# A hybrid encoder block on one core: half of the first feed-forward product by seven block products instead of eight

## The chip, the core and the metric

The kernel runs on one core of one Trainium2 chip. A core has TensorE (PE, matrix products into PSUM), VectorE (DVE), ScalarE (ACT), GpSimd (POOL) and SyncE (SP), each with a queue of instructions that it works through in order, and 16 DMA engines. The metric is the device time in microseconds, as the median of several runs.

## What is computed

One layer on x of 256 rows by 2048 columns, float32: a normalisation, two mixing branches (retention and latent attention) with gates, an output product, and then the feed-forward part that this case is about:

```python
z = _rmsnorm(h, norm_mlp_g[l]) @ w_up[l]          # 256 x 2048 by 2048 x 8192
h = h + jnp.square(jax.nn.relu(z)) @ w_down[l]    # 256 x 8192 by 8192 x 2048
...
return _rmsnorm(h, norm_f_g)
```

## The kernel before

**How a product is made.** TensorE multiplies float32 numbers in a form (`float32r`) that keeps fewer bits, so each operand is split: `hi` is the value cast to that form by ACT, `lo` is the rest, value minus hi, subtracted by DVE. A product is then three: hi by hi, hi by lo, lo by hi. `split` (L214 on) and `weights` (L145 to L153) do this; `weights` first loads a block of 128 x 1024 weights (512 KB) into a `raw` tile with a DMA in SP's queue, casts it on ACT (L151) and subtracts on DVE (L152). The pool `wp` has 5 raw, 4 hi and 4 lo tiles. Every weight is used once, so these steps accompany the whole kernel.

**The first feed-forward product** (w_up, L785 to L800) takes its input transposed and split: `hT`, 16 blocks of 128 rows, each with hi and lo for the 256 rows of x side by side. It is made in 64 units of 128 output columns. A unit (`t_unit`) keeps a block of weights stationary: `t_pass1` (L159) multiplies w-hi by hi and lo of hT together, 512 columns in one matmul, 16 of them; `t_pass2` (L163) multiplies w-lo by hi, 256 columns, 16 of them. The two halves of the 512-column result are added by `joined` (ACT copy L206, DVE add L207), and one DVE operation (L800) makes max(z, 0) times z and stores it in `hid`. All of hid stays in SBUF, in four tiles of 16 KB per partition, three of them from the pool `act` of six such tiles. The first two units are begun in halves, because the last quarter of hT is transposed (`mlp_turn`, tile `ht`, L764) while they run.

**The second product** (w_down, `down`, L814 to L816) is the other way round: blocks of hid (split into `dh` and `dl`) are stationary, and 512 columns of w_down move, three matmuls for each of eight PSUM banks (`pd`, tile dn), over 64 blocks. Its last two blocks are kept back and done bank by bank, while the finishing normalisation starts. `hn`, the residual, stays in SBUF from the output product (w_out, tile wo, L199 to L202) to the end.

**What sets the order.** The program is written as straight code; a scheduler then orders the instructions of each engine by a simulated timeline and gives tiles their buffers as they come free. Waits between engines are semaphores. PSUM has eight banks of 512 columns, four in the pool `mm` and four in `at`.

Of the kernel before, what the change touches and what calls it, by code (L numbers as in the profile page):

```python
# [27 lines left out]
CHUNK = 64  # L28
DFF = 8192
FT = DFF // P  # L30
EPS = 1e-6
QK_SCALE = float(192.0 ** -0.5)
LOWEST = -3.4e38
# [55 lines left out]
def block_kernel(ctx: ExitStack, tc: tile.TileContext, A):  # L89
    nc = tc.nc  # L90
    V, SC, G, PE = nc.vector, nc.scalar, nc.gpsimd, nc.tensor
# [3 lines left out]
    cp = ctx.enter_context(tc.tile_pool(name="cp", bufs=1))  # L95
# [4 lines left out]
    def big(name, dt=F32, shape=(P, KT, S)):  # L100
        return act.tile(list(shape), dt, tag="act16", name=name)
# [31 lines left out]
    def mmps(name):  # L133
        return pmm.tile([P, 512], F32, tag="mm", name=name)
# [4 lines left out]
    uid = [0]  # L139
# [56 lines left out]
    def n_tile(out, w, x, t, k0, nk, start, stop):  # L196
# [4 lines left out]
        for k in range(nk):  # L201
            PE.matmul(out, x.hi(k0 + k, ts), w[1][:, k], start=False, stop=stop and k == nk - 1)  # L202

    def join(out, ps):
        t = sm.tile([P, S], F32, tag="join", bufs=2, name="join")
        SC.copy(t, ps[:, S:])  # L206
        V.tensor_tensor(out=out, in0=ps[:, :S], in1=t, op=ALU.add)  # L207
# [22 lines left out]
    warm = cp.tile([P, 1], F32, name="warm")  # L230
    SC.activation(warm, halfpi, AF.Copy)

    cold = cp.tile([P, 512], BF16, name="cold")
# [5 lines left out]
    rctx = ExitStack()  # L239
    rope_pool = rctx.enter_context(tc.tile_pool(name="rope", bufs=2))  # L240
    ictx = ExitStack()
    ip = ictx.enter_context(tc.tile_pool(name="ip", bufs=1))

# [8 lines left out]
    x = Pair("x")  # L252
# [12 lines left out]
    for k0, k1 in zip(LEAD_CHUNKS, LEAD_CHUNKS[1:]):  # L265
        n = k1 - k0
        hs = slice(k0 % HK, k0 % HK + n)
        if k0 % HK == 0:
            wt = [[wtile(kind, [P, HK, P]) for kind in ("hi", "lo")] for j in range(3)]
        t, o = lead_at(k0)  # L270
# [12 lines left out]
        for ps, (hi, lo) in zip(firsts, wt):  # L283
            w = hi[:, hs], lo[:, hs]
# [31 lines left out]
    ident = con[:, C_ID : C_ID + P]  # L316
# [33 lines left out]
    rxb = cp.tile([P, S], F32, name="rxb")  # L350
    V.tensor_copy(rxb, pb[:, :S])

    tabs = []
# [1 line left out]
    def table(j):  # L355
        ang, kk = angs[j]
        sgn = vec[:, V_INV + 2 + j : V_INV + 3 + j]
        own = ip if j == 0 else cp
        cos = own.tile([P, S], F32, name=f"cos{j}")
        sin = own.tile([P, S], F32, name=f"sin{j}")  # L360
# [157 lines left out]

    with ExitStack() as mctx:
        cc = big("cc", F32R, shape=(P, 2 * LT, 2, S))  # L520
        kpe = cp.tile([P, S], F32, name="kpe")
        lp = ExitStack()
        lpool = lp.enter_context(tc.tile_pool(name="lp", bufs=1))

# [232 lines left out]
    def mlp_turn(c):  # L757
        for jj in range(2):
            pT = atps(f"ht{c}{jj}")
            for j in range(2):  # L760
                kt = 4 * c + 2 * jj + j
                for t in range(2):
                    o = j * S + t * P
                    PE.transpose(pT[:, o : o + P], hn[:, t, kt * P : (kt + 1) * P], ident)  # L764
                g = vec[:, V_MLP + kt : V_MLP + kt + 1]
                split(hT.hi(kt), hT.lo(kt), pT[:, j * S : (j + 1) * S], scale=g)
    hp = ctx.enter_context(tc.tile_pool(name="hp", bufs=1))
    ssh = cp.tile([P, 2, 4], F32, name="ssh")
# [13 lines left out]
    V.tensor_scalar(rh2, rh2, 1.0 / D, EPS, op0=ALU.mult, op1=ALU.add)  # L782
    V.reciprocal(rh2, rh2)

    up = [mmps(f"z{i}") for i in range(2)]  # L785
    for i in range(2):
        t_half(up[i], A["w_up"][i], hT, 0)
        if i == 0:
            mlp_turn(3)
    hid = [big(f"hid{i}") for i in range(3)]  # L790
    hid.append(hp.tile([P, KT, S], F32, name="hid3"))
# [11 lines left out]
    ssf = cp.tile([P, 2, 68], F32, name="ssf")  # L803
    rf = cp.tile([P, 2], F32, name="rf")
    LAST = 2

    def down(i, t, c, w, hs):
        (hi, lo), (dh, dl) = w, hs
        ts = slice(t * P, (t + 1) * P)
        ws = slice(c % 2 * 512, c % 2 * 512 + 512)  # L810
        out = pd[t][c]
        end = i == FT - 1
        mm = tc.keep_in_program_order if i >= FT - LAST else (lambda ins: ins)
        mm(PE.matmul(out, dh[:, ts], hi[:, ws], start=i == 0, stop=False))  # L814
        mm(PE.matmul(out, dh[:, ts], lo[:, ws], start=False, stop=False))  # L815
        mm(PE.matmul(out, dl[:, ts], hi[:, ws], start=False, stop=end))  # L816

    tail = []
    for i in range(FT):
        dh = hp.tile([P, S], F32R, tag="dh", bufs=3, name=f"dh{i}")  # L820
        dl = hp.tile([P, S], F32R, tag="dl", bufs=3, name=f"dl{i}")
        split(dh, dl, hid[i // KT][:, i % KT])
        ws = []
        for half in range(2):
            w = weights(A["w_down"][i][:, half * 1024 : (half + 1) * 1024], [P, 1024])
            ws.append(w)
            if i < FT - LAST:
                for t in range(2):
                    for c in (2 * half, 2 * half + 1):
                        down(i, t, c, w, (dh, dl))  # L830
        if i >= FT - LAST:
            tail.append((i, ws, (dh, dl)))
# [7 lines left out]
    def finish(t, c, lo, hi, n):  # L840
        h = hn[:, t, c * 512 + lo : c * 512 + hi]
        ps = pd[t][c][:, lo:hi]
        V.scalar_tensor_tensor(h, in0=ps, scalar=rh2[:, t : t + 1], in1=h, op0=ALU.mult, op1=ALU.add)
        junk = hp.tile([P, 512], F32, tag="junk", bufs=2, name=f"junk{t}{n}")
# [32 lines left out]
def _t_units(w):  # L877
    k, n = w.shape
    return np.ascontiguousarray(w.reshape(k // P, P, n // P, P).transpose(2, 1, 0, 3))


def _n_units(w):
    k, n = w.shape
    u = w.reshape(k // 512, 4, P, n // 512, 512).transpose(3, 0, 2, 1, 4)
    return np.ascontiguousarray(u.reshape(-1, P, 4, 512))


def _cols(v):
# [57 lines left out]
```

## Time and profile before

| | us |
|---|---|
| median of three runs | 1631.58 (1631.27 to 1631.89) |
| the profiled execution | 1632.22 |
| its span, first to last instruction | 1630.4 |
| w_up in it, first z matmul to first dn matmul | 915.5 to 1272.7 |
| w_down and the end | 1272.7 to 1630.4 |
| mean granted TensorE clock | 0.998 of full |

The page of the profile gives busy times by engine, the chain of work that ended last, and groups of instructions by line, engine and tile. In a group's name `z<-hT,hi` means that tile z is written from hT and hi. A duration is that of one instruction; matmuls overlap, so their pace is read from the distance of their starts in the timeline.

### The profile page before, as it was taken

What the parts mean: (1) busy time and instruction counts of PE and PEld (TensorE: products, weight loads), DVE (VectorE), ACT (ScalarE), POOL (GpSimd) and SP (SyncE); (2) the same over time, 40 slices, a digit from 0 to 9 for tenths busy, and PEclk for the clock granted to TensorE, in tenths of its full rate; (3) what the DMA queues carried; (4) which work ended last, traced back from release to release, by engine and by line L of the source; (5) the groups of instructions that cost most, each with busy time, mean ns of one, the idle gap of its engine ahead of it and who ended that gap; (6) DMA issues with size and microseconds to landing.
All of it is one profiled execution on the core that took longest, in us unless ns stands there. A gap on an engine that the chain in (4) does not pass through costs nothing.

```text
span 1630.4 us, 23041 instructions
## 1 busy us (share of the span) xinstructions
PE 1614.9 (99%) x8782; PEld 1398.8 (86%) x8782; DVE 996.2 (61%) x1491; ACT 809.7 (50%) x1249; POOL 49.5 (3%) x62
## 2 busy tenths in 40 slices
PE   8999999999999999999999999999999999999997
PEld 6888888888889889888888888888888888888886
DVE  7974588655556658666765555555555555555555
ACT  6544555544445556765545544444444444444444
POOL 7100000000000000000000000000000000000001
PEclk9999999999999999999999999999999999999999
DMA  8665544555556554325575555555555655555553
GB/s 306 200 233 193 187 156 166 169 192 186 190 170 203 190 191 146 125 94 176 186 246 187 174 193 188 192 189 186 191 192 184 223 194 192 193 193 195 192 194 112
DMA packets 84480, 304.46 MB, mean 187 GB/s; under 512 B 9360, under 2 KB 9488, under 8 KB 83600
## 3 DMA queue, kind: packets, MB, share of 16 engines
q1 hardware_dynamic: 84368, 302.98, 55.3%
q8 instruction: 69, 1.13, 0.3%
q14 instruction: 43, 0.35, 0.1%
HBM read 300.84 MB, written 2.10 MB: 186 GB/s over the span
## 4 chain that ended last, share of the span: by engine, by line
PE 97%; DVE 1%; issue 0%; DMA 0%; ACT 0%; POOL 0%; SPq 0%; DVEq 0%; POOLq 0%; ACTq 0%
PE z L159 14%; PE z L163 8%; PE dn L816 7%; PE dn L814 7%; PE dn L815 7%; PE rg L159 4%; PE yr L159 4%; PE gr L159 4%; PE gm L159 4%; PE mo L159 4%; PE qk L159 2%; PE gr L163 2%; PE yr L163 2%; PE gm L163 2%; PE rg L163 2%; PE mo L163 2%
## 5 line engine op out<-in xcount | busy, mean ns | idle before, releaser
L152 DVE TENSOR_TENSOR lo<-raw,hi 128x1024 fp32r<-128x1024 f32 (+2 forms) x562 | 666.0, 1204 | 521.6 <-ACT hi L151 248.3
L151 ACT CAST hi<-raw 128x1024 fp32r<-128x1024 f32 (+2 forms) x562 | 580.8, 1035 | 536.9 <-PE z L159 135.2
L159 PE MATMUL z<-hT,hi 128*128 128x512 f32 x1024 | 245.5, 391 | 0.0
L159 PEld LDWEIGHTS z<-hT,hi 128*128 128x128 f32 x1024 | 188.0, 188 | 36.1
L815 PE MATMUL dn<-lo,dh 128*128 128x512 f32 x512 | 199.2, 389 | 0.0
L816 PE MATMUL dn<-hi,dl 128*128 128x512 f32 x512 | 199.2, 389 | 0.0
L814 PE MATMUL dn<-hi,dh 128*128 128x512 f32 x512 | 198.9, 389 | 0.0
L163 PEld LDWEIGHTS z<-hT,lo 128*128 128x128 f32 x1024 | 131.6, 191 | 5.1
L163 PE MATMUL z<-hT,lo 128*128 128x256 f32 x1024 | 133.1, 283 | 0.0
L815 PEld LDWEIGHTS dn<-lo,dh 128*128 128x128 f32 x512 | 96.1, 188 | 20.1
L816 PEld LDWEIGHTS dn<-hi,dl 128*128 128x128 f32 x512 | 96.1, 188 | 19.9
L814 PEld LDWEIGHTS dn<-hi,dh 128*128 128x128 f32 x512 | 96.1, 188 | 19.8
L216 ACT CAST dh<-hid 128x256 fp32r<-128x256 f32 x64 | 26.0, 407 | 89.3 <-PE dn L815 89.3
L159 PE MATMUL mo<-my,hi 128*128 128x512 f32 x256 | 65.5, 396 | 0.4 <-DVE val L207 0.4
L159 PE MATMUL rg<-x,hi 128*128 128x512 f32 x256 | 64.0, 395 | 0.0
L159 PE MATMUL yr<-ry,hi 128*128 128x512 f32 x256 | 61.4, 391 | 0.0
L159 PE MATMUL gr<-x,hi 128*128 128x512 f32 x256 | 61.3, 391 | 0.0
L159 PE MATMUL gm<-x,hi 128*128 128x512 f32 x256 | 61.1, 391 | 0.0
L159 PEld LDWEIGHTS gm<-x,hi 128*128 128x128 f32 x256 | 47.0, 188 | 9.1
L159 PEld LDWEIGHTS gr<-x,hi 128*128 128x128 f32 x256 | 47.0, 188 | 9.0
L159 PEld LDWEIGHTS yr<-ry,hi 128*128 128x128 f32 x256 | 46.9, 188 | 9.0
L159 PEld LDWEIGHTS rg<-x,hi 128*128 128x128 f32 x256 | 46.2, 188 | 8.6
(271 smaller groups left out, 2239.1 us busy)
## 6 DMA issues: line engine op xcount, KB each, us to landing
raw<-w_up SPq DMA_DIRECT2D x128, 512.0 KB, 4.2
raw<-w_down SPq DMA_DIRECT2D x128, 512.0 KB, 4.3
raw<-w_rv SPq DMA_DIRECT2D x32, 512.0 KB, 4.5
raw<-w_rg SPq DMA_DIRECT2D x32, 512.0 KB, 4.5
raw<-w_gret SPq DMA_DIRECT2D x32, 512.0 KB, 4.3
raw<-w_ret_o SPq DMA_DIRECT2D x32, 512.0 KB, 4.6
raw<-w_gmla SPq DMA_DIRECT2D x32, 512.0 KB, 4.4
raw<-w_out SPq DMA_DIRECT2D x32, 512.0 KB, 3.7
```

Of the source, the lines that this page charges most:

```text
L151: SC.copy(hi, raw)
L152: V.tensor_tensor(out=lo, in0=raw, in1=hi.bitcast(F32), op=ALU.subtract)
L159: PE.matmul(out, w[0][:, k], x.both(k0 + k), start=start and k == 0, stop=False)
L163: PE.matmul(out[:, :S], w[1][:, k], x.hi(k0 + k), start=False, stop=stop and k == n - 1)
L216: SC.copy(hi, val)
L814: mm(PE.matmul(out, dh[:, ts], hi[:, ws], start=i == 0, stop=False))
L815: mm(PE.matmul(out, dh[:, ts], lo[:, ws], start=False, stop=False))
L816: mm(PE.matmul(out, dl[:, ts], hi[:, ws], start=False, stop=end))
```

## The change

The columns of w_up are cut in two. The second 4096 keep the old form (32 units). The first 4096 are made in 4 units (`SU`) of 1024 columns by a block scheme: input rows (two halves of 128), the depth (pairs of 128-row blocks) and output columns (two halves of 512) form 2 x 2 blocks, and seven products of sums of blocks stand for the eight products of blocks.

- **Sums of the input** (`Combos.make`): four combinations of the blocks of hT, made once, a quarter at a time, with DVE sums and a split; they take two of the six big tiles (`hc`).
- **A step** (`s_step`, 8 per unit, each a depth of 256): loads two halves of 512 KB of weights by SP (`sraw` from its own pool `zp`, and `raw`), makes four sums of weight blocks on DVE into `forms` (three instructions, L248 to L250), splits the four groups (7 blocks of 512 columns; tiles hi/lo and `shi`/`slo` with 5 buffers each), and runs 7 products with 3 matmuls each (L267 to L269). The input blocks are stationary and 512 columns of weights move. The seven results of a unit (tile `zs`) fill seven PSUM banks over its 8 steps.
- **The end of a unit** (`s_end`): one ACT copy and seven DVE operations turn the seven banks into the four blocks of the result, in `zo`. They lie with rows on partitions, so each is transposed by PE (tile `zt`, 64 transposes in all), in the midst of the next unit's steps.
- **Squares** (`square`): Relu and Square on ACT instead of one DVE operation, then a DMA in ACT's queue to `hid`, which now lies in DRAM (48 such DMAs). w_down reads hid back through POOL's queue, a pair of blocks at a time, three buffers (`hl`), the old-form blocks first.
- **Order**: three old units are begun in halves while the last quarter of hT and the last two sums are made; then steps and old units alternate, 32 steps among 27 old units, with two old units behind the last step. Old units take one `at` bank each.
- **Space**: hn is copied to DRAM after w_out (ACT's queue) and read back before w_down (SP's queue); some small tiles move to a pool that ends before the feed-forward part. The scratch for DMAs that POOL issues is set to 2048.

```diff
+    PRODUCTS = ((3, 0, 0), (4, 0, 1), (2, 1, 0), (5, 1, 1), (6, 2, 0), (1, 2, 1), (7, 3, 0))
...
+        def make(self, c):
+            if c % 2 == 0:
+                self.t.append(big(f"{self.name}{c // 2}", F32R, (P, KT // 4, 2, 4, P)))
+            x, q = wtile("raw", [P, 2, 2, 2, P]), wtile("raw", [P, 2, 4, P])
+            hi, lo = self.pair.span(4 * c, 4)
+            xs = x.rearrange("p j k t n -> p (j k) (t n)")
+            V.tensor_tensor(out=xs, in0=hi.bitcast(F32), in1=lo.bitcast(F32), op=ALU.add)
...
+            V.tensor_tensor(out=a2, in0=a11, in1=a12, op=ALU.subtract)
+            V.tensor_tensor(out=a5, in0=a11, in1=a21, op=ALU.subtract)
+            V.tensor_tensor(out=a6, in0=a2, in1=a21, op=ALU.subtract)
+            V.tensor_tensor(out=a4, in0=a6, in1=a22, op=ALU.add)
+            o = self.t[-1][:, c % 2 * 2 : c % 2 * 2 + 2]
+            split(o[:, :, 0], o[:, :, 1], q)
...
+    def s_step(qs, src, x, j, between):
+        rb = wtile("raw", [P, 2, 512])
+        ra = zp.tile([P, 2, 512], F32, tag="sraw", bufs=2, name=f"sraw{uid[0]}")
+        nc.sync.dma_start(ra, src[:, :2])
+        nc.sync.dma_start(rb, src[:, 2:])
+        fa, fb = (forms[:, 2 * (j % 2) + i] for i in range(2))
+        V.tensor_tensor(out=fa, in0=rb[:, 1:].to_broadcast([P, 2, 512]), in1=ra, op=ALU.add)
+        V.tensor_tensor(out=fb[:, 0], in0=fa[:, 0], in1=ra[:, 1], op=ALU.add)
+        V.tensor_tensor(out=fb[:, 1], in0=fb[:, 0], in1=rb[:, 0], op=ALU.add)
+        ws = []
+        for i, r in enumerate((ra, fa, fb, rb[:, :1])):
+            if i:
+                hi, lo = (
+                    zp.tile([P, r.shape[1], 512], F32R, tag=kind, bufs=5, name=f"{kind}{uid[0]}{i}")
+                    for kind in ("shi", "slo")
+                )
+            else:
+                hi, lo = (wtile(kind, [P, 2, 512]) for kind in ("hi", "lo"))
+            split(hi, lo, r)
+            ws.append((hi, lo))
+        for n, (f, i, o) in enumerate(PRODUCTS):
+            if n == 4:
+                between()
+            (ah, al), (hi, lo) = x.get(f, j), ws[i]
+            first, last = j == 0, j == SJ - 1
+            PE.matmul(qs[f], ah, hi[:, o], start=first, stop=False)
+            PE.matmul(qs[f], al, hi[:, o], start=False, stop=False)
+            PE.matmul(qs[f], ah, lo[:, o], start=False, stop=last)
+
+    def s_end(qs, out, tmp):
...
+        SC.copy(t3, qs[3])
+        tt(e, qs[6], t3)
+        tt(f, qs[2], e, ALU.subtract)
+        tt(c21, qs[4], f)
+        tt(c11, qs[5], f)
+        tt(e, e, qs[5], ALU.subtract)
+        tt(c12, qs[1], e)
+        tt(c22, qs[7], t3)
...
+        if c in (1, 2):
+            hc.make(c - 1)
...
-    for i in range(FT):
-        if i < 2:
-            pz = up[i]
-            t_half(pz, A["w_up"][i], hT, 1)
-        else:
-            pz = mmps(f"z{i}")
-            t_unit(pz, A["w_up"][i], hT)
-        z = joined(pz)
-        V.scalar_tensor_tensor(hid[i // KT][:, i % KT], in0=z, scalar=0.0, in1=z, op0=ALU.max, op1=ALU.mult)
+    def square(pair, n, val):
+        t = zp.tile([P, 2, S], F32, tag="hs", bufs=2, name=f"hs{pair}{n}")[:, : val.shape[1]]
+        SC.activation(t, val, AF.Relu)
+        SC.activation(t, t, AF.Square)
+        SC.dma_start(hid[pair][:, n : n + val.shape[1]], t)
...
+            keep = hidd.tile([P, 2, D], F32, name="hnkeep")
+            SC.dma_start(keep, hn)
+            hc.make(2)
+            forms = big("forms", shape=(P, 4, 2, 512))
...
+    for i in range(EARLY, FT - ST):
+        while done < SU * SJ and done * (FT - ST - EARLY - LATE) <= (i - EARLY) * SU * SJ:
+            next(steps)
+            done += 1
+        pz = atps(f"z{i}")
+        t_half(pz, A["w_up"][i], hT, 0)
+        t_half(pz, A["w_up"][i], hT, 1)
+        square((ST + i) // 2, i % 2, joined(pz).unsqueeze(1))
...
-    for i in range(FT):
+    for n, i in enumerate((*range(ST, FT), *range(ST))):
+        if n % 2 == 0:
+            hl = hp.tile([P, 2, S], F32, tag="hl", bufs=3, name=f"hl{i}")
+            G.dma_start(hl, hid[i // 2])
...
-        split(dh, dl, hid[i // KT][:, i % KT])
+        split(dh, dl, hl[:, i % 2])
```

More of the change, by code (lines that the diff above doesn't have):

```diff
@@ L30 @@
 FT = DFF // P
+SU = 4
+SJ = KT // 2
+ST = SU * 1024 // P
+EARLY, LATE = 3, 2
+SSF = 68
 EPS = 1e-6
@@ L204, in join, with tt @@
+    def s_end(qs, out, tmp):
+        t3, e, f = (tmp[:, i] for i in range(3))
+        c11, c12, c21, c22 = (out[:, t, c] for t in range(2) for c in range(2))
+        def tt(o, a, b, op=ALU.add):
+            V.tensor_tensor(out=o, in0=a, in1=b, op=op)
+        SC.copy(t3, qs[3])
[6 more added lines that the diff above has]
+        tt(c22, qs[7], t3)
     def join(out, ps):
@@ L231, in block_kernel @@
     SC.activation(warm, halfpi, AF.Copy)
-    cold = cp.tile([P, 512], BF16, name="cold")
+    rctx = ExitStack()
+    rope_pool = rctx.enter_context(tc.tile_pool(name="rope", bufs=2))
+    cold = rope_pool.tile([P, 512], BF16, tag="cold", bufs=1, name="cold")
     V.memset(cold, 0.0)
@@ L357, in table @@
         sgn = vec[:, V_INV + 2 + j : V_INV + 3 + j]
-        own = ip if j == 0 else cp
-        cos = own.tile([P, S], F32, name=f"cos{j}")
-        sin = own.tile([P, S], F32, name=f"sin{j}")
+        cos, sin = (
+            (ip if j == 0 else rope_pool).tile([P, S], F32, tag=f"{name}{j}", bufs=1, name=f"{name}{j}")
+            for name in ("cos", "sin")
+        )
         tc.keep_in_program_order(SC.activation(sin, ang, AF.Sin, scale=sgn))
@@ L520, in block_kernel @@
         cc = big("cc", F32R, shape=(P, 2 * LT, 2, S))
-        kpe = cp.tile([P, S], F32, name="kpe")
+        kpe = rope_pool.tile([P, S], F32, tag="kpe", bufs=1, name="kpe")
         lp = ExitStack()
@@ L767, in block_kernel @@
     hp = ctx.enter_context(tc.tile_pool(name="hp", bufs=1))
+    zctx = ExitStack()
+    zp = zctx.enter_context(tc.tile_pool(name="zp", bufs=1))
+    hidd = ctx.enter_context(tc.tile_pool(name="hidd", bufs=1, space=bass.MemoryType.DRAM))
+    hc = Combos("hc", hT)
     ssh = cp.tile([P, 2, 4], F32, name="ssh")
@@ L783, in block_kernel @@
     V.reciprocal(rh2, rh2)
-    up = [mmps(f"z{i}") for i in range(2)]
-    for i in range(2):
-        t_half(up[i], A["w_up"][i], hT, 0)
+    hid = [hidd.tile([P, 2, S], F32, name=f"hid{i}") for i in range(FT // 2)]
+    zo = big("zo", shape=(P, 2, 4, 512))
+    def square(pair, n, val):
[3 more added lines that the diff above has]
+        SC.dma_start(hid[pair][:, n : n + val.shape[1]], t)
@@ new lines, in s_units, with turn @@
+    def s_units():
+        turns = []
+        for u in range(SU):
+            qs = {f: (mmps if f in (3, 4, 2, 5) else atps)(f"zs{u}{f}") for f in range(1, 8)}
+            for j in range(SJ):
+                s_step(qs, A["w_up_s"][u, j], hc, j, turns.pop(0) if turns and j else lambda: None)
+                yield
+            s_end(qs, zo[:, 0].rearrange("p (t c) n -> p t c n", t=2), zo[:, 1])
+            def turn(u, jj):
+                pT = atps(f"zt{u}{jj}")
+                for j in range(2):
+                    kt = 2 * jj + j
+                    for t in range(2):
+                        o = j * S + t * P
+                        src = zo[:, 0, 2 * t + kt // 4, kt % 4 * P : kt % 4 * P + P]
+                        PE.transpose(pT[:, o : o + P], src, ident)
+                square(4 * u + jj, 0, pT.rearrange("p (j n) -> p j n", j=2))
+            turns = [lambda u=u, jj=jj: turn(u, jj) for jj in range(4)]
+        for fn in turns:
+            yield
+            fn()
@@ L788, in block_kernel @@
+    forms = None
+    steps = s_units()
+    early = [atps(f"z{i}") for i in range(EARLY)]
+    for i, pz in enumerate(early):
+        t_half(pz, A["w_up"][i], hT, 0)
         if i == 0:
             mlp_turn(3)
-    hid = [big(f"hid{i}") for i in range(3)]
-    hid.append(hp.tile([P, KT, S], F32, name="hid3"))
-    for i in range(FT):
-        if i < 2:
-            pz = up[i]
-            t_half(pz, A["w_up"][i], hT, 1)
-        else:
-            pz = mmps(f"z{i}")
-            t_unit(pz, A["w_up"][i], hT)
-        z = joined(pz)
-        V.scalar_tensor_tensor(hid[i // KT][:, i % KT], in0=z, scalar=0.0, in1=z, op0=ALU.max, op1=ALU.mult)
+            keep = hidd.tile([P, 2, D], F32, name="hnkeep")
+            SC.dma_start(keep, hn)
+            hc.make(2)
+            forms = big("forms", shape=(P, 4, 2, 512))
@@ new lines, in block_kernel @@
+    for i, pz in enumerate(early):
+        t_half(pz, A["w_up"][i], hT, 1)
+        square((ST + i) // 2, i % 2, joined(pz).unsqueeze(1))
+        if i == 0:
+            hc.make(3)
+    done = 0
+    for i in range(EARLY, FT - ST):
[3 more added lines that the diff above has]
+        pz = atps(f"z{i}")
+        t_half(pz, A["w_up"][i], hT, 0)
+        t_half(pz, A["w_up"][i], hT, 1)
+        square((ST + i) // 2, i % 2, joined(pz).unsqueeze(1))
@@ L802, in block_kernel @@
+    for _ in steps:
+        pass
+    hn = big("hn2", shape=(P, 2, D))
+    nc.sync.dma_start(hn, keep)
+    zctx.close()
+    jp = ctx.enter_context(tc.tile_pool(name="jp", bufs=1))
     pd = [[(mmps if t == 0 else atps)(f"dn{t}{c}") for c in range(4)] for t in range(2)]
-    ssf = cp.tile([P, 2, 68], F32, name="ssf")
+    ssf = cp.tile([P, 2, SSF], F32, name="ssf")
     rf = cp.tile([P, 2], F32, name="rf")
@@ L885, in _n_units, with _s_steps @@
     return np.ascontiguousarray(u.reshape(-1, P, 4, 512))
+def _s_steps(w):
+    k, n = w.shape
+    b = w.reshape(k // 256, 2, P, n // 1024, 2, 512)
+    q = np.stack([b[:, 0, :, :, 1], b[:, 1, :, :, 0], b[:, 1, :, :, 1], b[:, 0, :, :, 0]], axis=3)
+    return np.ascontiguousarray(q.transpose(2, 0, 1, 3, 4))
 def _cols(v):
@@ L935 @@
     }
-    nc = bacc.Bacc("TRN2", target_bir_lowering=False, num_devices=1)
+    nc = bacc.Bacc("TRN2", target_bir_lowering=False, num_devices=1, dynamic_dma_scratch_size=2048)
     A = {
```

31 lines of the change are left out of this document (22 added, 9 removed).

## The prediction

> **What bounds the kernel now.** I read the page first: busy shares, then the chain that ended last.
>
> ```profile
> span 1630.4 us, 23041 instructions
> PE 1614.9 (99%) x8782; PEld 1398.8 (86%) x8782; DVE 996.2 (61%) x1491; ACT 809.7 (50%) x1249; POOL 49.5 (3%) x62
> PE 97%; DVE 1%; issue 0%; DMA 0%; ACT 0%; POOL 0%; SPq 0%; DVEq 0%; POOLq 0%; ACTq 0%
> ```
>
> PE carries 97% of the chain, so a matmul less is time less, until another engine becomes the bound. Next, the timeline of PE in the stage that changes (w_up, tile z); the columns are start, length and count.
>
> ```profile
> 1003.55 2.08 PE L163 MATMUL z<-hT,lo 128*128 128x256 f32 x16
> 1005.46 3.82 PE L159 MATMUL z<-hT,hi 128*128 128x512 f32 x16
> 1009.11 2.08 PE L163 MATMUL z<-hT,lo 128*128 128x256 f32 x16
> 1011.03 1.32 PE L159 MATMUL z<-hT,hi 128*128 128x512 f32 x5
> ```
>
> From start to start a unit takes 1011.03 - 1005.46 = 5.57 us: 16 matmuls of 512 columns in 3.65 (0.228 each) and 16 of 256 in 1.92. Then the timeline of PE at the start of w_down, whose matmuls are built as the new ones are (512 columns, a new stationary each time):
>
> ```profile
> 1274.05 0.39 PE L814 MATMUL dn<-hi,dh 128*128 128x512 f32 x1
> 1274.27 0.39 PE L815 MATMUL dn<-lo,dh 128*128 128x512 f32 x1
> 1274.50 0.39 PE L816 MATMUL dn<-hi,dl 128*128 128x512 f32 x1
> 1274.73 0.39 PE L814 MATMUL dn<-hi,dh 128*128 128x512 f32 x1
> ```
>
> Three starts later is 0.68 us on: 0.2267 each. Last, what DVE has left: busy time by stretch (columns: PE, PEld, DVE, ACT, POOL, granted clock, DMA share, GB/s), and DVE's timeline in a w_up unit.
>
> ```profile
> 41.00:82.00 41.00, 41.00 (x237) 36.18 (x236) 39.42 (x71) 21.94 (x29) 4.89 (x6) 1.00 0.61 202
> 1000.00:1272.70 272.70, 272.70 (x1570) 241.01 (x1569) 152.91 (x197) 121.30 (x147) 0.00 (x0) 1.00 0.56 189
> ```
>
> ```profile
> 1004.76 2.36 DVE L152 TENSOR_TENSOR lo<-raw,hi 128x1024 fp32r<-128x1024 f32 x2 [2.41 <-PE z L163]
> 1007.04 0.42 DVE L207 TENSOR_TENSOR val<-z,join 128x256 f32<-128x256 f32 x1
> ```
>
> In w_up DVE has 56% to do and waits for PE (2.41 us a unit). In 41 to 82 it is busy 96% of the time and PE still has no gap: DVE can run nearly full without holding PE up. Two lo subtractions last 2.36 us where one lasts 1.223 (the w_up and w_down rows), so back to back one takes 1.137. I use 1.137 for 1024 elements, 0.60 for 512 (row of hn<-wo, 0.687, less the same 0.086) and 0.36 for 256.
>
> **PE, counted.** Removed: 32 of 64 w_up units, 32 x 5.57 = 178.2 us. Added, from the order of instructions as built: 4 units x 8 steps x 7 products x 3 matmuls = 672 of 512 columns, 672 x 0.2267 = 152.3. Added too: 64 transposes of finished s values (zt). PE's timeline in w_out gives their price, by the old ht transposes:
>
> ```profile
> 882.05 0.39 PE L200 MATMUL wo<-hi,mg 128*128 128x512 f32 x1
> 882.29 0.60 PE L764 MATMUL ht<-con,hn 128*128 128x128 f32 x4
> 882.64 0.71 PE L202 MATMUL wo<-lo,mg 128*128 128x512 f32 x2
> ```
>
> From 882.05 to 882.64 lie a matmul (0.227) and four transposes, 0.09 each; 64 x 0.09 = 5.8. Balance on PE: -178.2 + 152.3 + 5.8 = **-20.1 us**.
>
> [...]
>
> **DVE, counted.** A step adds: form sums 1 x 1024 and 2 x 512, lo parts 3 x 1024 and 1 x 512: 4 x 1.137 + 3 x 0.60 = 6.35 us, against 21 x 0.2267 = 4.76 on PE. A unit left in the old form needs 2 x 1.137 + 0.36 = 2.63 (its square moves to ACT), against 5.57. The end of an s unit adds 7 x 0.60 = 4.2. Between the first and the last s product lie 32 steps, 27 old units and 3 ends: DVE 203.2 + 71.0 + 12.6 = 286.8, PE 152.3 + 150.4 + 4.4 (48 transposes) = 307.1. So PE stays the bound, but DVE's share goes from 56% to 93%. The mean hides the shape, so I summed both queues, in their built order, from the first z matmul. Up to the worst place (the lo of a form in the fourth step of the second s unit) DVE has 74 x 1.137 + 43 x 0.60 + 26 x 0.36 + 0.6 = 119.9 us queued; PE has 176 x 0.228 + 176 x 0.1194 + 235 x 0.2267 + 12 x 0.09 = 115.5 ahead of the matmul that needs it. DVE is 4.4 late there, less about 2 of work that it can finish beforehand: **+2.4**. Some 80 us on (third s unit) it is 196.2 against 195.8, level; from then on steps are sparser and DVE leads by 17 to 20 us. So for 200 us every gap of DVE is a gap of PE; afterwards none is.
>
> How many gaps? Each lo follows an ACT cast. The row nearest is w_down's dl, which waits 39.6 us in 61 times, 0.65 each, for ACT's cast; but there DVE has nothing else queued, here it has. Bounds: 0 (41 to 82 us, no gaps) and 0.65 for each of the some 20 steps and 18 units in the critical 200 us, 25 us. I take 0.2 each, nearer to nothing since the order puts 1.1 to 7 us of other DVE work between a form and its lo: 24 x 0.2 = 4.8 by the worst place, so 2.4 + 4.8 = **+7.2** there (by 195 us: 0.4 - 2 + 7.6 = 6.0, less, so not added).
>
> **ACT, DMA, POOL.** ACT in the stretch: a step 3 x 0.95 + 0.52 = 3.4 (row of the casts, 1.05, less 0.1 back to back), an old unit 2 x 0.95 + 0.30 + Relu 0.31 + Square 0.40 + issue of its DMA 0.39 (SP's out rows, 333 to 431 ns) = 3.3, 12 turns at 1.5: 109 + 89 + 18 = 216 of 307, 70%. Not the bound; hidden behind PE; with that cover gone its price is DVE's gaps above. Weights: the same 32 MB as before; with 8 MB of hid written, some 215 GB/s against 189, and the page has slices of 246 and 306. The copy of hn to DRAM and back lies beside 16 us of early units; hn<-x, as large, lands in 8.8 us; nothing, or up to 5 if forms' buffer comes free late. The hid reads go through POOL, which moves no data before, so no row prices them. Two of them feed casts queued on ACT among w_up's (dh), and subtractions on DVE (dl); behind each wait every weight cast of the stretch. From below nothing; from above a landing as long as the longest here, con's 13.4 us, less the some 6 that the order leaves. I take **+2**, by the 2.5 us of a 256 KB out. In w_down three buffers hold a read two pairs of units, 22 us, ahead: nothing.
>
> The four hc sums add 4 us of DVE each; two lie beside w_out, where DVE is 56% busy, two beside the early units and are in the sum above. At the handover to w_down ACT has some 8 us of squares and issues ahead of the third block's casts while PE has 11 us of prepared matmuls, but the four banks of the last transposes come free one by one: **+1**.
>
> Sum: -20.1 + 7.2 + 2 + 1 = -9.9. The profiled execution took 1632.22 (span 1630.4 plus 1.8 around it): 1622.3; the median of the runs shown is 0.6 below it: **1621.7 us**.
>
> **Rivals.**
> - *All of it hidden.* For it: the stretch 41 to 82. Against: ACT had 54% there, 70% here. -20.1: 1611.5. Chance 0.15.
> - *Each DVE operation costs its whole duration* (1.223, 0.687, 0.42), because waits on ACT and on its own results break the pairs. At 195 us DVE has 122 x 1.223 + 75 x 0.687 + 33 x 0.42 = 214.6 against 195.8 on PE: +18.8 - 2, with +2 and +1 a net of -0.3: 1631.3, no change. Against: in 41 to 82 neighbours overlap. Chance 0.10. [...]
> - *Slower: DVE and ACT take turns.* A form goes DVE, ACT, DVE, and both queues are in order: if one cast per step and per old unit comes late by w_down's 0.65, that is 38 x 0.65 = 24.7 in the critical 200 us; with 0.4 - 2, +2 and +1 the net is 24.7 - 1.6 + 3 - 20.1 = +6.0: 1637.6. It decides once DVE is less than about 90% busy there. For it: squares, joins and DMA issues stand in ACT's queue between casts. Chance 0.20.
> - *Transposes at their whole 272 ns*, each waiting alone: 64 x 0.18 = 11.6 more: 1633.3. Against: the ht starts. Chance 0.03.
> - *The POOL reads land late*, with DVE and ACT queued behind: 7 us for each of the two, 14 instead of 2: 1633.7. Chance 0.12.
>
> My forecast keeps 0.40. Range: 1610 (all hidden, 1.5 for the rows) to 1641 (the slower rival with its waits an eighth longer). What a measurement here tells from no change is 0.2%, 3.3 us. Faster takes the forecast, the hidden rival and a part (0.10) of the others, where only some of their price falls due: 0.65; same 0.09; slower 0.26.
>
> **What would show it.** After: w_up's stretch some 347 us long (357.2 before, from 915.5 to 1272.7); 672 matmuls 0.227 apart; PE's gaps in its first 200 us some 8 us, put down to DVE's lo or ACT's hi, and hardly any later; DVE above 90% there; no gap in w_down. I am wrong if the gaps pass 20 us, if they go on through the last s unit, or if PE waits for POOL's reads.

## The result, and the profile after

The changed kernel takes **1635.0 us** (median of 20 runs, 1629.8 to 1639.4); the kernel before, on the same chips, 1631.5 (1631.2 to 1632.3). The ratio is 1.0019, 95% interval [1.0012, 1.0026]: 3.5 us slower, little but clear of no change, where 1621.7, 10 us faster, was forecast. The profiled execution took 1632.87, 2.2 us less than the median.

The page of the changed kernel: the span, the busy times and the shares of the chain.

```profile
span 1631.1 us, 22859 instructions
PE 1604.4 (98%) x8494; PEld 1373.6 (84%) x8494; DVE 1118.5 (69%) x1607; ACT 887.3 (54%) x1385; POOL 67.7 (4%) x94
PE 92%; DVE 4%; DMA 2%; issue 1%; ACT 1%; POOL 0%; SPq 0%; DVEq 0%; POOLq 0%; ACTq 0%
```

PE issues 288 matmuls fewer and its share of the chain falls from 97% to 92%. The rest has come to DVE, DMA and ACT. The chain runs back from a wait of PE through all that the wait hung on, so these shares are larger than the time that PE stood still: 26.7 us (span less busy time) for 15.5 before. Busy time by stretch (columns: PE, PEld, DVE, ACT, POOL, granted clock, DMA share, GB/s) shows that the added idle time is in w_up:

```profile
914.50:1130.00 215.50, 208.29 (x1049) 174.36 (x1048) 197.56 (x233) 140.14 (x199) 2.44 (x4) 0.99 0.66 225
1130.00:1271.00 141.00, 135.65 (x701) 114.23 (x700) 118.02 (x134) 90.83 (x128) 0.00 (x0) 1.00 0.67 231
```

From the first z matmul (914.48) to the first of dn (1272.87) pass 358.4 us; before, 357.2. PE stands idle some 7 us in the first 215 and 5 in the last 141, where nothing was forecast. DVE is 92% busy in the first stretch, as forecast, and only 84% in the second.

A finer measure is needed, since a busy PE can be slow (a stretch below has its starts 0.43 us apart for 0.227). I went through PE's timeline of this stretch and took, from each start to the next, what exceeds the counted pace (0.2275 us for 512 columns, between the prediction's 0.228 and 0.2267; 0.1194 for 256; 0.09 for a transpose). This **loss** is 1.2 us in the kernel before and **21.7 us** in the changed one. Of the 20.1 us that PE had less to do nothing is left. Idle time named by the profile is 12.4 us of the loss. The longest waits (PE, the stretch; columns: us in total, times, longest):

```profile
PE z L164 <- ACT hs L880: 3.2, 4, 1.6
PE zs L267 <- ACT shi L299: 3.1, 2, 2.9
PE z L164 <- DVE val L290: 2.9, 3, 1.7
PE zs L269 <- DVE slo L300: 1.8, 2, 1.2
```

Two of the four were in my sum: a form's cast or lo part that comes late. The other two were not. There z waits for the Relu of turned values (hs) or for the join of the unit before (val): it waits for its **PSUM bank**. With 0.2 us before zt these waits come to 6.3 us. Four banks of `mm` and three of `at` hold the seven products of an s unit for all its eight steps. One of eight banks is left, and z and zt go through it in turn. One such wait, in the timeline of all engines:

```profile
1170.50 0.39 PE L269 MATMUL zs<-lo,hc 128*128 128x512 f32 x1
1170.60 0.36 ACT L289 COPY join<-z 128x256 f32<-128x256 f32 x1
...
1171.01 1.22 DVE L157 TENSOR_TENSOR lo<-raw,hi 128x1024 fp32r<-128x1024 f32 x1
...
1172.14 0.42 DVE L290 TENSOR_TENSOR val<-z,join 128x256 f32<-128x256 f32 x1
...
1172.61 0.50 PE L164 MATMUL z<-hT,hi 128*128 128x512 f32 x1 [1.72 <-DVE val L290]
```

The unit before had its last matmul at 1169.3. Its join stood behind other casts in ACT's queue (1170.60), then behind a lo part in DVE's (1172.14). The bank was held for 3.3 us after PE was done with it; six zs matmuls covered part of that and 1.72 us stayed open.

The longest gap has a second price. PE's timeline behind it:

```profile
948.35 0.62 PE L269 MATMUL zs<-slo,hc 128*128 128x512 f32 x2
951.82 0.77 PE L267 MATMUL zs<-shi,hc 128*128 128x512 f32 x1 [2.85 <-ACT shi L299]
952.39 0.63 PE L268 MATMUL zs<-shi,hc 128*128 128x512 f32 x1
952.82 0.63 PE L267 MATMUL zs<-shi,hT 128*128 128x512 f32 x1
```

After 2.85 us of idleness the starts lie 0.43 us apart instead of 0.227, until 955.35; the granted clock from 951.80 to 955.40 is 0.53. That adds some 1.7 us to the gap. The cast that PE waited for stood in ACT's queue behind a first cast of hid, which waited for its read through POOL (ACT's timeline):

```profile
948.90 0.41 ACT L299 CAST dh<-hl 128x256 fp32r<-128x256 f32 x1 [4.65 <-DMA hl<-hid]
```

### The profile page after: what moved, and what is told of

Same layout as the page of the kernel before. It is cut to its first block, busy times and chain, and to the rows that moved or that the text cites. A ratio compares the mean times of both kernels' runs of the same rounds, so it can differ in the third digit from the quotient of the medians.

```text
span 1631.1 us, 22859 instructions
## 1 busy us (share of the span) xinstructions
PE 1604.4 (98%) x8494; PEld 1373.6 (84%) x8494; DVE 1118.5 (69%) x1607; ACT 887.3 (54%) x1385; POOL 67.7 (4%) x94
## 4 chain that ended last, share of the span: by engine, by line
PE 92%; DVE 4%; DMA 2%; issue 1%; ACT 1%; POOL 0%; SPq 0%; DVEq 0%; POOLq 0%; ACTq 0%
PE dn L954 7%; PE dn L952 7%; PE dn L953 7%; PE z L164 6%; PE rg L164 4%; PE yr L164 4%; PE gr L164 4%; PE gm L164 4%; PE mo L164 4%; PE z L168 3%; PE zs L269 2%; PE zs L267 2%; PE zs L268 2%; PE qk L164 2%; PE gr L168 2%; PE yr L168 2%
## 5 line engine op out<-in xcount | busy, mean ns | idle before, releaser
L157 DVE TENSOR_TENSOR lo<-raw,hi 128x1024 fp32r<-128x1024 f32 (+2 forms) x498 | 592.1, 1201 | 377.1 <-ACT hi L156 247.4
L156 ACT CAST hi<-raw 128x1024 fp32r<-128x1024 f32 (+2 forms) x498 | 512.8, 1032 | 425.7 <-PE dn L954 96.3
L164 PE MATMUL z<-hT,hi 128*128 128x512 f32 x512 | 129.7, 394 | 7.3 <-ACT hs L880 3.2
L164 PEld LDWEIGHTS z<-hT,hi 128*128 128x128 f32 x512 | 93.0, 188 | 28.2 <-ACT hs L880 4.8
L953 PEld LDWEIGHTS dn<-lo,dh 128*128 128x128 f32 x512 | 96.1, 188 | 20.1
L952 PEld LDWEIGHTS dn<-hi,dh 128*128 128x128 f32 x512 | 96.1, 188 | 19.8
L299 ACT CAST shi<-forms 128x1024 fp32r<-128x1024 f32 x64 | 67.1, 1048 | 23.5 <-DVE forms L248 15.0
L300 DVE TENSOR_TENSOR slo<-forms,shi 128x1024 fp32r<-128x1024 f32 x64 | 77.9, 1217 | 0.2
L299 ACT CAST dh<-hl 128x256 fp32r<-128x256 f32 x64 | 26.1, 407 | 89.3 <-PE dn L953 84.6
L168 PEld LDWEIGHTS z<-hT,lo 128*128 128x128 f32 x512 | 69.9, 190 | 5.0
L168 PE MATMUL z<-hT,lo 128*128 128x256 f32 x512 | 71.6, 282 | 0.0
L960 POOL DMA_DIRECT2D hl<-hid x32 | 17.8, 556 | 1032.7 <-DVE dl L300 540.2
```

Of the source, the lines that this page charges most:

```text
L156: SC.copy(hi, raw)
L157: V.tensor_tensor(out=lo, in0=raw, in1=hi.bitcast(F32), op=ALU.subtract)
L164: PE.matmul(out, w[0][:, k], x.both(k0 + k), start=start and k == 0, stop=False)
L168: PE.matmul(out[:, :S], w[1][:, k], x.hi(k0 + k), start=False, stop=stop and k == n - 1)
```

## The experiments

Theory 1 at the outset: PE was counted rightly, and what is lost are waits, for the bank, for late casts and for the POOL read. Theory 2: loads come late. The rival to both: PE's work itself is dearer than counted. All times are medians; before lay between 1631.4 and 1631.7 in every comparison. The loss is that of the profiled execution alone. Runs marked * leave something out or put two products into one bank, so their output is not the reference's.

| run | what is different from the changed kernel | us | ratio to before, interval | loss in w_up |
|---|---|---|---|---|
| changed | | 1635.0 | 1.0019 [1.0012, 1.0026] | 21.7 |
| e1* | few forms | 1630.3 | 0.9993 [0.9984, 1.0002] | 19.8 |
| e2 | first dh, dl late | 1640.8 | 1.0058 [1.0045, 1.0071] | 32.7 (to 1290; profiled 1644.2) |
| e3 | SU = 2 | 1689.7 | 1.0354 [1.0340, 1.0368] | 68.9 |
| e4 | SU = 0 | 1633.8 | 1.0013 [1.0004, 1.0022] | 2.9 |
| e5* | product 7 in product 1's bank: two spare banks | 1619.2 | 0.9926 [0.9914, 0.9938] | 8.5 |
| e6 | rb in buffers of its own | 1640.8 | 1.0055 [1.0035, 1.0075] | 27.7 |
| e7 | e6 and turns between units | 1641.9 | 1.0061 [1.0049, 1.0073] | 28.6 |
| e8* | e5 and e6 | 1619.1 | 0.9925 [0.9912, 0.9937] | 6.9 |
| e9 | z and zt in half banks | 1664.2 | 1.0199 [1.0185, 1.0213] | 47.9 (to 1323, where the last transposes end) |
| e10* | e1 and e5 | 1615.5 | 0.9904 [0.9890, 0.9917] | 4.0 |
| e11* | e3 and e5 | 1628.7 | 0.9983 [0.9975, 0.9992] | 7.2 |
| e12 | product 7 apart: two spare banks, complete | **1619.4** | **0.9923 [0.9909, 0.9937]** | 8.7 |
| e13 | join copied out by ACT | 1632.8 | 1.0001 [0.9992, 1.0009] | 22.9 |
| e14 | SU = 0, z in one bank | 1793.5 | 1.0992 [1.0977, 1.1007] | 162.0 |
| e15 | e12 and e13 | 1624.3 | 0.9951 [0.9938, 0.9963] | 8.4 |

**Was PE counted right?** (e1)

```diff
-        fa, fb = ...                          # and the three sums into forms
-        for i, r in enumerate((ra, fa, fb, rb[:, :1])):
+        for i, r in enumerate((ra, rb)):
...   # the products on formed blocks take loaded blocks instead
```

> The form sums of w_up's blocks and the casts and lo parts of the two formed pairs are left out (the seven products use the two loaded pairs of blocks instead), so the output is not the reference's; PE's instructions stay as they are. DVE has 2.3 us to do in a step for 6.35, ACT 1.9 for 3.4. Theory 1 (the count of PE was right, and the 21.7 us that PE loses in the stretch are waits): the waits put down to DVE's slo and to late loads go; what stays is at most the waits at the bank that z and zt share (6.6 us of them in the trace of the changed kernel) and at the read through POOL (some 5). So 1631.5 - 20.1 + 1.5 to 10 = 1613 to 1621. Rival (PE itself is dearer than counted: transposes at 272 ns, or matmuls not 0.227 apart): 1628 or more. If DVE's load is not what matters, 1633 to 1636 as the changed kernel.

1630.3, outside what theory 1 gave and in the range of its rival, yet not for the rival's reason. The matmuls are as far apart as counted (time less loss gives 1611.4 us, the count 1611.4); the loss is 19.8 us, nearly all that the changed kernel has, with DVE relieved of two thirds of a step. So DVE's load is worth 4.8 us here and is not the main cause. Of the waits that are left, 7.7 us are at the bank (z for hs 3.8 us, z for val 2.1, zt for val and hs 1.8) and 3.0 are for casts.

**A second bank.** (e5) Product 7 adds into product 1's bank.

```diff
-            qs = {f: ... for f in range(1, 8)}
+            qs = {f: ... for f in range(1, 7)}
+            qs[7] = qs[1]
...   # first and last now by the shared bank
```

> Product 7 is accumulated into product 1's bank, so a unit in seven products holds six banks and z and zt have two to share for one; the output is not the reference's, PE's work and that of the other engines stay as they are. In the trace of the changed kernel PE's waits at the one bank (z after ACT's Relu hs or after DVE's val, zt after val) come to 8 us of the 21.7 lost in the stretch; with few forms (the first experiment) they are 8 of 19.8. Theory 1 (the one spare bank is a cause of its own): 6 to 8 us less than the changed kernel's 1635, 1627 to 1629. Rival (PE then only waits for the next late cast): 1632 to 1635.

1619.2: **15.8 us less** than the changed kernel (13.7 between the profiled executions), more than twice the 6.3 us of waits that its profile names at the bank. PE's waits in its stretch:

```profile
PE zs L267 <- ACT shi L299: 1.7, 3, 0.8
PE z L164 <- ACT hi L156: 0.6, 1, 0.6
PE z L164 <- DVE hT L303: 0.6, 1, 0.6
PE z L164 <- DVE val L290: 0.6, 1, 0.6
```

Of these four, two (hi and hT) belong to the start of the stretch. Not only z's waits shrink (6.3 us to 0.6), but those for casts too (4.9 to 2.1), though ACT and DVE have the same to do; and no stretch at low clock is left (1.00 up to 1130 us, for 0.99 in the changed kernel). In the first s unit the built order suggests how. From 969 us on, z's matmuls come in whole units with one bank; with two, up to 1022 us PE's order puts z matmuls in pieces between zs matmuls, so that PE has something else ready when a cast is late. By the end of that unit the loss is 7.8 us with one bank, 3.3 with two. Afterwards both orders have z in whole units nearly everywhere, and the loss still grows by 14.0 us with one bank and 5.1 with two: there it is mainly the waits at the bank and PE's slower starts behind them (0.11 to 0.14 us later than counted after a named wait of z or zs in the changed kernel, but for the gap of 2.85 us).

**What does DVE cost, once there are banks?** (e10, the two edits above together)

> The first and the fifth experiment together: the forms, their casts and lo parts left out, and product 7 in product 1's bank; the output is not the reference's. PE's count puts the floor at 1631.5 - 20.1 = 1611.4, plus the 1.5 us of waits at the start of the stretch: 1612 to 1614. If DVE's load is what remains in the fifth experiment (1619.2, 7.8 above the count), it shows as the difference of the two, 5 to 7 us. If what remains is something else (POOL reads, loads, matmuls dearer than counted): 1617 to 1620 here too.

1615.5, 1.5 us above what was expected of the floor, and DVE's load shows as 3.7 us where 5 to 7 were expected. The steps add up in medians: the count 1611.4, other small losses 4.1 (e10), DVE's and ACT's forms 3.7 (e5 less e10), the bank 15.8 (changed less e5): 1635.0. Taken in the other order the forms are 4.8 (changed less e1) and the bank 14.7 (e1 less e10): the two overlap by 1 us.

**Old units against one bank.** With SU = 2 there are fewer products to put between 43 old units (e3); with SU = 0 none (e14), and e4 is the same with four banks.

> SU = 2: a quarter of the first feed-forward product in seven block products, in 16 steps between 44 old units. PE's balance is half, -10.0. DVE has 16 x 6.35 + 43 x 2.63 + 4.2 = 219 us to do beside 317 on PE (69%), so nothing of DVE should be late. Theory 1 (waits at the shared bank and at the POOL read stay, DVE's go): -10.0 + half of 6.6 + 5 = -2, 1628 to 1631. By the working of the prediction (DVE's lateness is the loss, the rest 3 us): 1624 to 1625. Rival (each step has a loss of its own, whatever the density): loss and gain halve alike, 1632 to 1634.

> SU = 0: no unit in seven products; all 64 units in the old form, with the squares on ACT, hid written to DRAM and read back through POOL, hn kept in DRAM, and the buffers as in the changed kernel. It prices the second half of the change alone. Theory 1: PE counts as before (64 units), DVE and ACT have slack, the read through POOL may cost one wait: 1631.5 + 0 to 4. Rival (the detour by DRAM or the shared cast buffers cost on their own, at the handover or in w_down): 1638 or more.

> The fourth experiment (SU = 0, 1633.8: no steps at all) with the 61 later units of w_up all in one bank. DVE is 55% busy, there are no steps and no forms, so this is the price of one bank where PE has nothing else to run: at each unit PE waits for ACT's copy (0.37) and DVE's add (0.42) and the signals between, some 1.1 us, 61 x 1.1 = 67, and if PE runs at half clock after each gap, 1.7 us more of each: 1700 to 1805. If gaps of this size cost only themselves: 1695 to 1705. If the bank costs nothing there: 1634.

e3 took 1689.7, far outside everything expected: half the change costs sixteen times as much. e4 took 1633.8: hid through DRAM, the copy of hn and the POOL reads cost 2.1 us together. Most of it is in w_up, where units now run by halves: a row of matmuls of the first kind takes some 0.013 us more than its count with 16 (mean in the kernel before) and 0.013 to 0.022 with 8 (changed kernel, e14), and there are 128 rows for 66. e14, in the timeline of all engines:

```profile
1102.68 1.11 PE L168 MATMUL zz<-hT,lo 128*128 128x256 f32 x8
...
1103.84 0.37 ACT L289 COPY join<-zz 128x256 f32<-128x256 f32 x1
1103.96 1.23 DVE L157 TENSOR_TENSOR lo<-raw,hi 128x1024 fp32r<-128x1024 f32 x1 [1.56 <-ACT hi L156]
1105.11 0.42 DVE L290 TENSOR_TENSOR val<-zz,join 128x256 f32<-128x256 f32 x1
...
1105.58 0.73 PE L164 MATMUL zz<-hT,hi 128*128 128x512 f32 x2 [1.78 <-DVE val L290]
```

Each of 59 named waits is some 1.78 us, not the 1.1 expected: what DVE's add (1105.11) needs is ready at 1104.2, but the add stands behind a lo part. Busy time by stretch shows the clock behind the gaps (the number after POOL's):

```profile
1105.58:1110.02 4.44, 4.44 (x16) 3.88 (x17) 0.00 (x0) 1.86 (x3) 0.00 (x0) 0.62 0.42 149
1110.02:1114.70 4.68, 2.94 (x18) 2.41 (x16) 2.79 (x3) 1.32 (x2) 0.00 (x0) 1.00 0.29 112
1122.38:1126.63 4.25, 4.25 (x17) 3.74 (x18) 0.00 (x0) 1.86 (x3) 0.00 (x0) 0.65 0.42 154
```

After 25 of the 59 gaps the trace has half the clock for 3.4 us. Of the loss of 162 us, 105 are the gaps themselves and some 43 the half clock (25 x 3.4 / 2); the rest is mostly the slower first starts behind each gap (0.13 us by the median). With one bank the whole loss per old unit after the first three is 0.75 us at SU = 4 (29 units), 1.5 at SU = 2 (45) and 2.7 with no steps (61): the more products lie between old units, the smaller it is.

Does the bank explain e3 as well? (e11: SU = 2 with e5's edit)

> The third experiment (SU = 2, 1689.6) with product 7 in product 1's bank; the output is not the reference's. If the bank is what made it so slow (44 old units, each waiting for the join of the one before): 1631.5 - 10 + 2 to 6 = 1624 to 1628. If it is the loads of the steps, which come late between old units: 1650 or more.

1628.7, 61 us below e3 and 0.7 above what was expected. In e3 the profile had put 23.3 us on zs waiting for ACT's shi and only 15.3 on the bank; one bank more removes nearly all of both (a loss of 7.2 for 68.9).

**The POOL reads.** (e2)

```diff
+        if n < 4:
+            tc.keep_in_program_order(SC.copy(dh, hl[:, i % 2]))
+            tc.keep_in_program_order(V.tensor_tensor(out=dl, ...))
```

> The first four casts dh and subtractions dl of w_down are pinned behind w_up's last instructions on ACT and DVE; nothing else is changed. Theory 1 (the read of hid through POOL held up ACT's queue for 4.6 us and with it the cast that PE waited 2.85 us for, and PE then ran some microseconds at half clock): 3.4 + 1.7 us less than the changed kernel, some 1630, with no gap over 1.5 us in the first 100 us of the stretch and a granted clock of 1.00 there. Rival (DVE is behind anyway and the same wait comes back at the next late form): within 1.5 us of the changed kernel's 1635.

The gap that began at 949 fell from 2.85 us to 1.92 only: another late form stood right behind. In exchange the casts now come after the last squares, which wait for the two hs buffers to be written out, and the handover opens (timeline of ACT and PE):

```profile
1280.30 0.60 ACT L880 ACTIVATE hs<-zt 128x512 f32<-128x512 f32 x1 [0.97 <-DMA hid<-hs]
...
1282.41 0.79 PE L952 MATMUL dn<-hi,dh 128*128 128x512 f32 x1 [8.07 <-ACT dh L964]
```

1640.8, outside both ranges: what my prediction took for a hazard, the early reads, is worth 1 us and saves 8 in the gap of this profile (5.8 net in medians).

**Late loads.** (e6 and e8, and with the turns e7)

```diff
-        rb = wtile("raw", [P, 2, 512])
+        rb = zp.tile([P, 2, 512], F32, tag="srb", bufs=2, ...)
...   # formed pairs' casts: 3 buffers, the small one 2, for 5 of both
```

> The second pair of blocks of a step gets two buffers of its own (rb no longer takes one of the five raw buffers that the old units' loads go round), paid for by three buffers for one formed pair's casts where there were five for all, and two small ones. Theory 2 (loads are late: rb and the old units' loads wait in SP's queue until DVE frees a raw buffer, land 4 to 4.7 us later, and the first form of a step waits for it; DVE waited 20 us for such loads in the stretch): DVE's wait at L248 for DMA falls from 20 us to under 5, and the time by 4 to 8 us, 1627 to 1631. Rival (DVE is the bound, loads only take its idle time): 1633 to 1636.

> The fifth and the sixth together (product 7 in product 1's bank, rb with buffers of its own); the output is not the reference's. If bank and loads are the two causes and add up: 1635 - 7 - 6 = 1622, within 3. If they overlap (the same gap has both behind it): 1626 to 1630. If DVE's 93% is a third cause that shows as soon as these are gone: 1628 to 1632, with PE's waits in the first 200 us put down to DVE's slo and val.

> As the last, and all four turns of a finished unit come before the first step of the next, in banks that this unit has given up, so that z has the spare bank to itself from the second step on; a complete kernel. If both theories hold, both prices go: 1619 to 1625, faster than both kernels. If PE waits for the end of the unit on DVE instead (7 operations queued behind casts), one wait of 2 to 4 us for each of three units: 1627 to 1632. If neither cause is real: 1633 to 1637.

Theory 2 finds no support. e6 is slower than the changed kernel (1640.8). DVE's wait for DMA at the first form went from 20.2 us to 11.0, not under 5, and the cast buffers given up for it are a second difference, so e6 alone settles little. e8 says more: with two banks the same edit changes nothing (1619.1 for 1619.2), though this wait falls from 11.2 us in e5 to 5.4. So late loads seem to fill DVE's idle time and not to make it; with one bank and all cast buffers kept this was not tested. e7 (1641.9, slower than anything expected) found no way round the bank: PE waited 4.1 us for the end of a unit on DVE (zo) and 7.5 us for the Relu of turned values before it could write their banks again.

**How to get the bank.** First by halving z (e9):

```diff
+            PE.matmul(out, w[0][:, k], x.hi(kk), start=kk == 0, stop=False)   # out: 256 columns
+            PE.matmul(out, w[0][:, k], x.lo(kk), start=False, stop=False)
...   # z and turned values alternate between the halves of one bank; no join
```

> A complete kernel: an old unit among the steps puts its hi, lo and lo-of-weights products into the same 256 columns (three matmuls of 256 columns for one of 512 and one of 256), so that z needs half a bank and no join, and z and the turned values (now 256 at a time) alternate between the two halves of the one spare bank. PE pays 29 x 16 x (2 x 0.1194 - 0.228) = 5.0 us more than the changed kernel; ACT and DVE lose 29 joins. If the single spare bank is the main cause, its price (15.8 us by the fifth experiment) goes nearly all: 1635 + 5 - 13 to -16 = 1624 to 1627, faster than both kernels. If halves of one bank cannot be read and written side by side, or the wait for the bank only moves: 1634 to 1640.

1664.2, far above both ranges. In its timeline of all engines, the two pairs of transposes go to different halves:

```profile
1154.40 0.38 ACT L889 ACTIVATE hs<-zz 128x256 f32<-128x256 f32 x1 [3.17 <-PE zz L908]
...
1154.83 0.33 PE L908 MATMUL zz<-con,zo 128*128 128x128 f32 x1 [0.24 <-ACT hs L889]
```

PE starts on the second half when ACT has read the first (1154.78). The program as built makes PE wait for the read of the other half (0.24 us in the last row), so a half is no bank of its own here, and there are now twice as many turned values to pass through it. No run here shows whether the program orders the two by bank or by tile.

Then by taking DVE out of the bank's release (e13):

```diff
-        square(..., joined(pz).unsqueeze(1))
+        square(..., joined_act(pz).unsqueeze(1))   # ACT copies 512 columns, DVE adds from the copy
```

> One spare bank as in the changed kernel, but among the steps ACT copies the whole bank of z out (512 columns, some 0.6 us, for the half in 0.37), and DVE adds the halves from there, so the bank comes free without DVE. If it is DVE's queue that holds the bank (the add stands behind casts' lo parts): 4 to 8 us less than the changed kernel, 1627 to 1631. If the bank is held by ACT's queue and by the turned values as much: within 2 us, 1633 to 1637.

1632.8: 2.2 us less, at the edge of "within 2" (its profiled execution shows no gain: a loss of 22.9). DVE's part in holding the bank, less what ACT's longer copies cost, is small against 15.8. And last by needing one bank less (e12): the steps make six products, product 7 follows the unit's last step.

```diff
-    PRODUCTS = (..., (1, 2, 1), (7, 3, 0))
+    PRODUCTS = (..., (1, 2, 1))
...
+            qs[7] = atps(f"zs{u}7")
+            for jj in range(SJ // 2):
+                hi, lo = weights(A["w_up_s"][u, 2 * jj : 2 * jj + 2, :, 2].rearrange(...), [P, 2, 512])
...   # for two depths each: the three matmuls with hc.get(7, j)
```

> A complete kernel with two spare banks: the steps run six products; product 7 of a unit (needed for one output block alone) is run after the unit's last step, 24 matmuls in a row in a bank of its own, from its blocks loaded once more (2 MB a unit) and cast by the old route. PE, DVE and ACT have as much to do as in the changed kernel, DMA 8 MB more. If the spare bank is the main cause: 1619 to 1623, as the fifth experiment's 1619.2 plus a wait or two for the end of a unit; faster than both kernels. If the fifth experiment gained by something else that product 7 in product 1's bank changed: 1631 to 1635.

> The twelfth and thirteenth together, a complete kernel. If holding banks is the cause and the join's DVE part a share of it: 1 to 3 us below the twelfth, 1617 to 1621. If two banks are enough: equal to the twelfth within 1 us. If ACT's longer copies (29 x 0.23 us) delay casts: 1 to 3 us above it.

1619.4 us, a ratio of 0.9923 [0.9909, 0.9937]: a complete kernel that beats both. Its busy times over w_up, first z to first dn:

```profile
914.50:1259.50 345.00, 341.29 (x1762) 289.27 (x1761) 312.67 (x350) 227.79 (x314) 2.43 (x4) 1.00 0.75 258
```

The stretch takes 345 us for 358, with DVE as busy (312.7 of 345, 91%) and DMA at 258 GB/s for 227: a DVE as full as this and 8 MB more to load did not keep the gain away. It is also the test of e5: the bank is won by another edit, and the time is the same. e15 came out at 1624.3, 4.9 above e12 where 1 to 3 were expected at most. Its profiled execution is its fastest (1619.6) and shows none of the difference; why the others are slower is open.

## Why the prediction was wrong

**The step that failed: the sum has no term for PSUM.** I counted instructions, queues and loads. Of banks I looked only at the handover to w_down (+1) and not at the stretch, although the count is one line of arithmetic: seven products in eight banks leave one for 32 old units and 16 turns, where the old units had four. Before, with four banks in turn, a join could take three units' time unseen (PE was busy for all 357.2 us of w_up); here its whole way through the queues of ACT and DVE lies between one unit and the next. That is 15.8 us (e5, e12), four fifths of what was to be gained. What the bank does is shown by the runs; how far another order of the same work in one bank would do better is not (e7 was the one attempt).

**PE's balance, -20.1: right.** Time less loss gives 1631.0 for the kernel before (1632.2 - 1.2) and 1611.2 for the changed one; likewise 1611.4 (e1), 1610.7 (e5), 1611.5 (e10) and 1611.2 (e12). So 19.5 to 20.3 us less work; the pace of a matmul (0.2275 us for 512 columns) and 0.09 a transpose hold. The rival of 272 ns a transpose (the mean duration of ht in the trace of before) is out: it needs 11.6 us, and the whole loss of e10 is 4.0.

**DVE's gaps, +7.2: the mechanism was there, the size too large.** DVE was over 90% busy in the first 200 us, as said. Its forms, casts included, cost 3.7 us with banks to spare (e5 less e10) and 4.8 with one (changed less e1). The slower rival, DVE and ACT taking turns, gave 1637.6, close to the measured time, but by another mechanism: without most of DVE's load 1630.3 is left, with one bank more 1619.2. Nearer still by number is the rival of late POOL reads (1633.7); that is chance too, since e2 puts the early reads at about 1 us, not 14.

**POOL's reads, +2, and the handover, +1:** about 1 (the gap in e2) and near nothing. "Nothing" for ACT's added work held only while a bank was free: squares and joins in ACT's queue are part of what holds it. The detour by DRAM and the units by halves cost 2.1 in e4, but most of that belongs to its 128 rows of matmuls; the changed kernel has 64, about as many as before, so little of it is due here.

**What I had named as signs:** the stretch 347 us, measured 358.4. The gaps did not pass the 20 us that I had named: they are 12.4, and 21.7 only with the slow pace behind them. In the first 200 us they are 6.3, near the forecast 8; the 6.1 behind that were not forecast, and that they go on through the last s unit is the sign that came true. PE's wait for a POOL read, the third, came once, through ACT's queue, as a part of the 2.85 us. The second sign points to the cause: from 1150 on DVE has time to spare, and the gaps there (1.6, 1.7, 0.2, 0.7, 0.7, 0.4 us) are all z waiting for the bank.

## What to carry to other kernels

When a change holds accumulators longer, count the PSUM banks that are left for everything that runs between, and follow one value from its last matmul through each queue to the release of its bank, with these queues as full as the change makes them. Two banks for interleaved work were enough here and one was not (e12's 1619.4 us for 1635.0); a product that only one output needs can be run apart to win the second. The waits that a profile names at a scarce buffer were less than half of its price here (6.3 us of 15.8): it also took away other work with which PE could have covered late casts (waits of 4.9 us for 2.1 in e5), each gap was followed by some slower starts (0.11 to 0.14 us after most), and some cost clock (0.53 after the gap of 2.85 us).

## What the runs showed of the hardware

Gaps of under 2 us were followed by slow stretches in two runs. In e14 gaps of 1.78 us, one every 8.3 us on average, were followed in 25 of 59 cases by half the clock for 3.4 us (0.62 to 0.65 in the stretches shown above). In e1, behind two gaps of 1.11 and 0.72 us within 2.5 us, eight matmuls of each kind took 4.43 us from 1078.32, 2.78 by the count. In the changed kernel one gap of 2.85 us was followed by a clock of 0.53 (951.80 to 955.40), and single ones of 1.62 and 1.72 us were not followed by a lower one, as busy time by stretch shows (the number after POOL's):

```profile
956.00:1270.00 314.00, 305.82 (x1558) 257.35 (x1557) 279.46 (x318) 204.74 (x283) 1.66 (x3) 1.00 0.65 223
```

What decides which gaps are followed by a lower clock was not shown: 34 of e14's were not. The spread goes with the clock: the 20 runs of the changed kernel go from 1629.8 us at a mean clock of 0.998 to 1639.4 at 0.994, while those of the kernel before lie within 1.1 us. Which gaps differ between these runs is not known, since one alone was profiled.
